# Gated RMS norm of the SSD branch: squares added on GpSimd and summed over channels once per half of the tokens, in a newly ordered instruction list

## The chip, the cores and the metric

The kernel runs on one core of a Trainium2 chip. Its time is the device time of one execution in microseconds (us). The five engines of the core (TensorE, VectorE, ScalarE, GpSimd, and SyncE for DMA issue) each run their own instruction list in order and wait for each other through semaphores. In the rows below they are called PE (with PEld for its weight loads), DVE, ACT, POOL and SP.

## The reference, cut to what matters

One layer of a hybrid network: Mamba-2 (SSD) heads and latent-attention heads side by side, a shared output projection, and a SwiGLU feed-forward part. It runs over 512 prompt tokens and 64 sample tokens, in float32. The piece that is changed is the gate of the SSD output and its RMS norm over 512 channels:

```python
y = y + p['d_skip'].astype(jnp.float32)[:, None] * xh.astype(jnp.float32)
y = y.reshape(b, T, SSD_WIDTH) * jax.nn.silu(z.astype(jnp.float32))
y_ssd = rmsnorm(y, p['ssd_norm']).astype(x.dtype)

def rmsnorm(x, w):
    xf = x.astype(jnp.float32)
    y = xf * lax.rsqrt(jnp.mean(xf * xf, axis=-1, keepdims=True) + EPS)
    return (y * w.astype(jnp.float32)).astype(x.dtype)
...
x = x + jnp.concatenate([y_ssd, o], axis=-1) @ p['w_out']
```

## The kernel before, in words

All activations lie transposed: channels on the 128 partitions, the 576 tokens (512 + 64) along the free axis. The 512 SSD channels are four tiles `xsd[:, 0..3]` of 128 x 576. The tokens are worked through in chunks of 128: chunks 0 to 3 are the prompt, chunk 4 is the 64 sample tokens. Large products are split into a high and a low float32r part and run as three matmuls of 288 columns each (`wh`/`wl` are the weights' parts); small ones run in float32, where the profile shows one matmul as two records.

The middle of the kernel, from about 95 to 215 us, has two stages that overlap. `ORDER_SSD` lists the steps of the first: `z0` to `z3` (projection of the gate, DVE line 476 reads its PSUM banks and R1), `a`, `e`, `b`, `s` (the chunk's transposes, decays, outputs, state), `g` (the gate of a chunk), `v` and `p`/`q`/`k` (values, queries and keys of head pairs). `ORDER_ATT` lists the second: `N` (the norm), `y0` to `y3` (the scaled and split operands `cat_y` of the output projection), `S`/`T`/`V` (scores, transposes, values of attention) and `F` (the part of the output projection that takes `cat_y`).

A gate (line 625) multiplies the chunk of `xsd` by `sz` on DVE (L629), squares it on ACT (L631), and sums the squares over channels on PE with a matrix of ones, into a bank of the three-bank PSUM pool `pp`. For chunks 0 to 3 the sums are packed: the 128 tokens are cut in four pieces of 32, and each piece's sums are written to 32 of the 128 partitions (L639, 16 matmuls of 32 x 32 per chunk); chunk 4 takes four matmuls of 64 columns (L636). ACT copies the result to 32 (64) columns of `ssy`, which is the buffer R1. So the norm's own arithmetic (line 815, `norm_half`, L186 to L193) runs on 192 columns in place of 576. After it, the factors have to be spread to all partitions again: four matmuls with columns of the identity (L821) and a copy of 512 columns (L825), and a 64-column copy on POOL (L818). The output `Ry` then scales `xsd` (L828), ACT writes the high part of `cat_y` (L157) and DVE the low part (L159).

The order of the instructions is not left to the order of the code. A table of numbers per engine (`ISSUE`) fixes the place of every instruction on PE, DVE, ACT, POOL and SP, and a table `PLACES` fixes which bank or buffer every tile of a pool takes.

Of the kernel before, what the change touches and what calls it, by code (L numbers as in the profile page):

```python
# [13 lines left out]
AF = mybir.ActivationFunctionType  # L14
# [5 lines left out]
P = 128  # L20
# [4 lines left out]
TH = T // 2  # L25
# [31 lines left out]
def hybrid_layer_kernel(ctx: ExitStack, tc: tile.TileContext, a, o):  # L57
# [394 lines left out]
    def bank(tag, name):  # L452
        return placed(psq if tag == "sc" else psh, [P, 512], F32, tag, name)
# [925 lines left out]
0202102121201021012012210021012101201210210120201201201201201202102102102102102102102102102102102102102102102102210120  # L1379
1202101  # L1380
# [16 lines left out]
653 657 665-667 639 689-690 668-674 640 691-704 675-676 661 677-679 705-709 658 680-681 710-712 682 644 659 683-688  # L1397
662 660 737-744 713-714 745-755 765 715-732 756-760 663 733 645-652 761 654 762 734 793 664 794 763 735 655 764 736
766-767 795-796 768-770 656 771-772 831 797-808 773-779 832 809-811 780-788 812 789-792 835 813-824 833 869-871
836-837 872 829 834 830 875 838 825-826 876 827 877 828 873-874 855-862 890 881-883 878 863 879 864-866 891 880  # L1400
887-888 867 894 884-886 868 889 895-896 926-927 897 892 928 893 929-931 898-899 839 900-904 840-844 905-909 845-852
910-913 853-854 914-921 938 947 939 922 940 923 941-942 924 943 925 932-934 948-956 935-936 957 937 958-960 993-995
944-946 1012-1013 996-997 1014 961-973 977-992 974-976 1015-1017 1002-1003 998 1004-1006 1018 999-1001 1019 1007-1011
1020-1023 1028 1024 1029 1035 1063 1051 1025-1027 1036 1064-1065 1039 1052-1053 1040-1041 1066 1054 1037 1067-1068
1055-1057 1030-1031 1069 1042-1043 1070 1044 1058-1059 1032 1060 1033 1071 1061-1062 1072 1034 1073-1074 1048-1049
# [12 lines left out]
1572-1582 1628 1647 1584 1583 1585-1590 1630 1621 1591 1622 1631 1592 1637 1593 1596-1599 1594-1595 1634 1600-1601
# [268 lines left out]
```

## Time and profile before

| what | value |
|---|---|
| median of 3 runs | 631.69 us (631.28 to 631.85) |
| profiled execution, its own time | 631.44 us |
| its span, first to last instruction | 629.5 us |
| mean granted TensorE clock | 0.997 of full speed (2.4 GHz) |
| busy: PE, DVE, ACT, POOL | 619.3, 553.6, 386.9, 75.5 us |

The span is what the trace shows; about 1.9 us of the execution's time lie around it. An engine's busy time is the union of its instructions' times, so a high share says that it always has something under way, and not by itself that it sets the end. Which engine sets the end of a stage is read from the chain of waits and from who waits for whom there.

### The profile page before, as it was taken

The numbers are of one execution on the slowest core, as the hardware profiler recorded it, in microseconds if no ns is written. First come the engines' busy times: TensorE is split into PE (matmuls) and PEld (weight loads), VectorE is DVE, ScalarE is ACT, GpSimd is POOL, SyncE is SP. The second block draws the span as 40 slices with busy tenths as digits, with TensorE's granted clock in tenths as the row PEclk, the third lists the DMA queues.
The fourth block names the chain that finished last, engine by engine and source line by source line (L and its number), as shares of the span: only waits on it lengthen the run. The fifth ranks groups of instructions, "written<-read, shape, count | busy, mean of one in ns | idle before, by whom it ended". The sixth has DMA issues, their size and how long they took to land.

```text
span 629.5 us, 12140 instructions
## 1 busy us (share of the span) xinstructions
PE 619.3 (98%) x4717; PEld 592.2 (94%) x4717; DVE 553.6 (88%) x979; ACT 386.9 (61%) x749; POOL 75.5 (12%) x113
## 2 busy tenths in 40 slices
PE   9999999999999999999999999999999999999995
PEld 9899999987787899999999999999999999999994
DVE  7899997899876799999999997799888998999676
ACT  7554335689767489756556565555665666644454
POOL 1323141011100000000012001100211011100023
PEclk9999999999999999999999999999999999999998
DMA  9512185223221223121376337460765265725105
GB/s 318 207 42 88 40 236 144 92 79 126 91 95 34 103 100 111 71 89 68 91 186 138 106 106 182 109 156 34 191 169 127 69 180 116 186 72 171 36 0 185
DMA packets 32889, 74.64 MB, mean 119 GB/s; under 512 B 3882, under 2 KB 11960, under 8 KB 32576
## 3 DMA queue, kind: packets, MB, share of 16 engines
q1 hardware_dynamic: 26688, 62.73, 30.6%
q0 software_dynamic: 5424, 10.57, 9.4%
q8 instruction: 37, 0.61, 0.4%
q10 hardware_dynamic: 720, 0.57, 0.3%
q14 instruction: 20, 0.16, 0.1%
HBM read 59.14 MB, written 4.15 MB: 101 GB/s over the span
## 4 chain that ended last, share of the span: by engine, by line
PE 83%; DVE 11%; DMA 3%; issue 2%; ACT 1%; SPq 0%; DVEq 0%; POOL 0%; ACTq 0%; POOLq 0%
PE ps_x L947 15%; PE ps_o L465 8%; PE ps_in L143 8%; PE ps_dx L1087 8%; PE ps_z L947 7%; PE ps_l L1157 4%; PE ps_y L947 4%; PE ps_dz L1087 4%; PE ps_first L143 3%; PE ps_z L465 3%; PE sc L726 3%; DMA db<-in_w_down 2%; PE ps_dy L1087 2%; PE ps_p L947 2%; PE ptp L748 1%
## 5 line engine op out<-in xcount | busy, mean ns | idle before, releaser
L947 PE MATMUL ps_x<-xop,wh_gu_S 128*128 128x288 f32 x504 | 120.0, 295 | 0.9 <-ACT u L1016 0.9
L947 PEld LDWEIGHTS ps_x<-xop,wh_gu_S 128*128 128x128 f32 x504 | 85.9, 188 | 1.6 <-ACT u L1016 1.4
L947 PE MATMUL ps_x<-xop,wl_gu_S 128*128 128x288 f32 x252 | 73.7, 295 | 0.0
L947 PE MATMUL ps_z<-xop,gu_a 128*128 128x288 f32 x252 | 57.4, 295 | 0.0
L127 ACT CAST wh_gu_S<-gu 128x1024 fp32r<-128x1024 f32 x44 | 46.0, 1052 | 16.3 <-PE ps_y L947 6.7
L128 DVE TENSOR_TENSOR wl_gu_S<-gu,wh_gu_S 128x1024 fp32r<-128x1024 f32 x44 | 53.2, 1217 | 0.9 <-ACT wh_gu_S L127 0.3
L1100 POOL DMA_DIRECT2D x<-db x16 | 14.9, 969 | 276.9 <-DVE x L1139 136.4
L947 PEld LDWEIGHTS ps_x<-xop,wl_gu_S 128*128 128x128 f32 x252 | 47.1, 188 | 0.1
L143 PE MATMUL ps_in<-xs,wh_in 128*128 128x288 f32 x256 | 45.8, 298 | 0.0
L947 PE MATMUL ps_z<-xop,wh_gu_S 128*128 128x288 f32 x168 | 42.8, 295 | 0.0
L947 PE MATMUL ps_y<-xop,wh_gu_A 128*128 128x288 f32 x168 | 42.2, 294 | 0.0
L947 PEld LDWEIGHTS ps_z<-xop,gu_a 128*128 128x128 f32 x252 | 41.8, 188 | 0.0
L947 PE MATMUL ps_x<-xop,wh_gu_A 128*128 128x288 f32 x168 | 40.2, 295 | 0.0
L143 PEld LDWEIGHTS ps_in<-xs,wh_in 128*128 128x128 f32 x256 | 37.8, 188 | 0.7 <-ACT wh_in L127 0.5
L127 ACT CAST wh_gu_A<-gu 128x1024 fp32r<-128x1024 f32 x22 | 23.1, 1051 | 17.3 <-PE ps_x L947 11.1
L465 PE MATMUL ps_o<-cat_y,wh_out 128*128 128x288 f32 x128 | 32.9, 331 | 0.0
L128 DVE TENSOR_TENSOR wl_gu_A<-gu,wh_gu_A 128x1024 fp32r<-128x1024 f32 x22 | 26.8, 1220 | 4.7 <-ACT wh_gu_A L127 2.3
L947 PEld LDWEIGHTS ps_z<-xop,wh_gu_S 128*128 128x128 f32 x168 | 29.4, 188 | 0.0
L947 PEld LDWEIGHTS ps_y<-xop,wh_gu_A 128*128 128x128 f32 x168 | 29.4, 188 | 0.1
L947 PEld LDWEIGHTS ps_x<-xop,wh_gu_A 128*128 128x128 f32 x168 | 28.7, 188 | 0.1
L143 PE MATMUL ps_in<-xs,wl_in 128*128 128x288 f32 x128 | 27.7, 295 | 0.0
L465 PE MATMUL ps_z<-xs,wh_z 128*128 128x288 f32 x128 | 26.8, 304 | 0.4 <-ACT cth L410 0.4
(610 smaller groups left out, 2005.5 us busy)
## 6 DMA issues: line engine op xcount, KB each, us to landing
gu<-in_w_gu SPq DMA_DIRECT2D x44, 512.0 KB, 4.6
db<-in_w_down SPq DMA_DIRECT2D x16, 512.0 KB, 4.6
x<-db POOLq DMA_DIRECT2D x16, 288.0 KB, 6.1
x<-dc POOLq DMA_DIRECT2D x16, 288.0 KB, 3.8
wr_in<-in_w_in SPq DMA_DIRECT2D x8, 512.0 KB, 5.2
wr_out<-in_w_out SPq DMA_DIRECT2D x8, 512.0 KB, 3.3
cumb<-cumD SPq DMA_DIRECT2D x5, 512.0 KB, 6.0
x<-in_xT SPq DMA_DIRECT2D x2, 1152.0 KB, 6.2
```

The costliest lines, as they stand in the source:

```text
L127: act.copy(hi, raw)
L128: dve.tensor_tensor(lo, raw, hi.bitcast(F32), ALU.subtract)
L143: pe.matmul(ps[:m, hf, :n], w, x[:, hf * n : (hf + 1) * n], start=start and k == 0 and i == 0, stop=stop and k == last and i == 2,)
L465: pe.matmul(ps[:, :n], w, x[:, cols], start=not onto and k == 0 and i == 0, stop=onto or (k == len(terms) - 1 and i == 2), skip_group_chec ...
L726: pe.matmul(s[:, :nk], qs[:, j, q0 : q0 + P], ks[:, j, :nk], start=True, stop=True)
L748: pe.transpose(pp[:, k : k + P], prs[p, i][:, j, b * P : b * P + P], ident)
L947: pe.matmul(ps, p, q, start=not onto and first and kp == kps[0] and j == 0, stop=onto or (last and kp == kps[-1] and j == 2), skip_group_c ...
L1087: pe.matmul(ps, l, r, start=not onto and k == 0 and j == 0, stop=onto or (k == n - 1 and j == 2), skip_group_check=onto,)
L1100: pool.dma_start(x2[t], v, accum_op=ALU.add)
L1157: pe.matmul(ps, w, x[:, cols], start=first and not onto and k == 0 and i == 0, stop=onto or (last and k == len(terms) - 1 and i == 2), ski ...
```

## The change

A gate keeps its product and its squares. The four squared channel tiles are then added on GpSimd: one instruction adds tiles 0 and 1 to tiles 2 and 3 (128 x 256 for a full chunk), a second adds the two results into the chunk's own columns of `ssy` (128 x 128). The matmuls and the copy of the gate are gone. `norm_y` sums `ssy` over channels with one float32 matmul of 288 columns per half of the tokens, and does the norm's arithmetic on each half, 288 columns wide, straight from PSUM and with the result on all partitions. The spread is gone.

```diff
@@ gate(c)
         act.activation(q, yv, AF.Square)
-        n = L // 4 if c < 4 else L
-        ps = bank("pp", f"ps_g{c}")[:, :n]
-        for t in range(4):
-            if c == 4:
-                pe.matmul(ps, ones, q[:, t], start=t == 0, stop=t == 3)
-                continue
-            for j in range(4):
-                pe.matmul(ps[32 * j : 32 * j + 32], ones[:, :32], q[:, t, j * n : j * n + n], start=t == 0, stop=t == 3)
-        act.copy(ssy[:, n * c : n * c + n] if c < 4 else ssy[:, P : P + n], ps)
+        pool.tensor_tensor(q[:, :2], q[:, :2], q[:, 2:], ALU.add)
+        pool.tensor_tensor(ssy[:, tk], q[:, 0], q[:, 1], ALU.add)
@@ norm_y()
-        R = ssy[:, : P + TS]
-        norm_half(R, R, 512)
-        pool.tensor_copy(Ry[:, TP:], R[:, P:])
-        ps = bank("pp", "ps_ry")
-        for j in range(4):
-            pe.matmul(
-                ps.rearrange("p (c j n) -> p j c n", c=4, j=4)[:, j], ident[:, 32 * j : 32 * j + 1].to_broadcast([P, P]),
-                R[:, :P].rearrange("p (c n) -> p c n", c=4), start=True, stop=True,
-            )
-        act.copy(Ry[:, :TP], ps)
+        y0, nv, u = (tmp(f"nr_y{z}") for z in "yvu")
+        for hf in range(2):
+            cols = slice(hf * TH, (hf + 1) * TH)
+            ps = bank("pp", f"ps_g{hf}")[:, :TH]
+            pe.matmul(ps, ones, ssy[:, cols], start=True, stop=True)
+            act.activation(y0[:, cols], ps, AF.Ln, scale=1.0 / 512, bias=epsb)
+            dve.tensor_scalar(nv[:, cols], ps, -0.5 / 512, -0.5 * EPS, ALU.mult, ALU.add)
+            act.activation(y0[:, cols], y0[:, cols], AF.Exp, scale=-0.5)
+            act.activation(u[:, cols], y0[:, cols], AF.Square)
+            dve.tensor_tensor(u[:, cols], u[:, cols], nv[:, cols], ALU.mult)
+            dve.scalar_tensor_tensor(Ry[:, cols], u[:, cols], 1.5, y0[:, cols], ALU.add, ALU.mult)
@@ ISSUE (PE, DVE, ACT, POOL) and PLACES["pp"]: new numbers
-0-3 7 18 28 4 8 5 9 6 10 26-27 11 29 12-17 20-22 19 23-25 31 30 32-42 54 56 58 60 55 57 59 61 43-48 50-53 49 62-75 77
+0-3 7 18 28 4 8 5 9 6 10 26-27 11 29 12-17 20-22 19 23-25 31 30 32-42 60 62 64 66 61 63 65 67 43-48 54-56 49-52 57 53
```

The lists of `ORDER_SSD`, `ORDER_ATT` and `ORDER_FFN` are as before, and so is SP's order. The new tables move instructions only in the two stages from about 95 to 215 us; the feed-forward part keeps its order. Three places follow, before and after.

PE, where the output of chunk 0 (`ps_y0`) is followed by that of chunk 1 (`ps_y1`); `ps_x2` and `ps_b2` are transposes of chunk 2, `ps_v` value tiles, `ps_s0` the state of chunk 0, `ps_g4` the sums of chunk 4's gate. Before:

```order
L573 MATMUL ps_y0_1572<-E0_1458,xdt0_1320 64x128 x8
L528 MATMUL ps_x2_1607<-ident_84,xsd_112 128x128
L657 MATMUL ps_v0_1675<-wh_uv_1670,ckv_377 128x512
L657 MATMUL ps_v0_1675<-wl_uv_1671,ckv_377 128x512
...
L657 MATMUL ps_v2_1686<-wl_uv_1671,ckv_377 128x512
L636 MATMUL ps_g4_1589<-ysq4_1587,ones_86 128x64
L657 MATMUL ps_v2_1686<-wh_uv_1670,ckv_377 128x512
L636 MATMUL ps_g4_1589<-ysq4_1587,ones_86 128x64
L657 MATMUL ps_v1_1680<-wl_uv_1671,ckv_377 128x512
L657 MATMUL ps_v1_1680<-wh_uv_1670,ckv_377 128x512
L573 MATMUL ps_y1_1642<-E1_1496,xdt1_1484 64x128 x8
```

After:

```order
L573 MATMUL ps_y0_1572<-E0_1458,xdt0_1320 64x128 x8
L573 MATMUL ps_y1_1622<-E1_1496,xdt1_1484 64x128 x8
L528 MATMUL ps_x2_1603<-ident_84,xsd_112 128x128
L507 MATMUL ps_s0_1591<-xw0_1468,bt0_1327 128x256
L650 MATMUL ps_v0_1655<-wh_uv_1650,ckv_377 128x512
L507 MATMUL ps_s0_1591<-xw0_1468,bt0_1327 128x256
```

Chunk 1's outputs stand directly behind chunk 0's; nine value matmuls, the state matmuls of chunk 0 and the gate sums of chunk 4 stood between them.

DVE, from the end of the norm to the first low part of `cat_y`; `sc` are score banks, `pr` probabilities, `qs` the queries of pair 1, and L828 (L822 after) scales a tile of `xsd` by `Ry`. Before:

```order
L711 RECIPROCAL sm_2028<-sm_2028 128x2
L676 COPY qs1_384<-ps_q1_0_1943 64x288
L716 TENSOR_SCALAR pr_0_2_2029<-pr_0_2_2029,sm_2028 128x384
L676 COPY qs1_384<-ps_q1_1_1958 64x288
L711 RECIPROCAL sm_2042<-sm_2042 128x2
L716 TENSOR_SCALAR pr_0_0_2043<-pr_0_0_2043,sm_2042 128x128
L709 TENSOR_REDUCE mx_2054<-sc0_s_2051 128x1
L828 SCALAR_TENSOR_TENSOR xsd_112<-xsd_112,par_81,Ry_1957 128x576
L709 TENSOR_REDUCE mx_2065<-sc1_3_0_2061 128x1
L828 SCALAR_TENSOR_TENSOR xsd_112<-xsd_112,par_81,Ry_1957 128x576
L709 TENSOR_REDUCE mx_2065<-sc1_3_1_2063 128x1
L159 TENSOR_TENSOR cat_y0_1998<-xsd_112,cat_y0_1998 128x576
```

After:

```order
L819 SCALAR_TENSOR_TENSOR Ry_1889<-nr_yu_1901,nr_yy_1899 128x288
L702 TENSOR_REDUCE mx_1976<-sc0_0_1_1974 128x1
L822 SCALAR_TENSOR_TENSOR xsd_112<-xsd_112,par_81,Ry_1889 128x576 x2
L704 RECIPROCAL sm_1977<-sm_1977 128x2
L669 COPY qs1_384<-ps_q1_1_1890 64x288
L704 RECIPROCAL sm_1963<-sm_1963 128x2
L709 TENSOR_SCALAR pr_0_0_1978<-pr_0_0_1978,sm_1977 128x128
L669 COPY qs1_384<-ps_q1_0_1875 64x288
L709 TENSOR_SCALAR pr_0_2_1964<-pr_0_2_1964,sm_1963 128x384
L159 TENSOR_TENSOR cat_y0_1933<-xsd_112,cat_y0_1933 128x576
```

Two of the four scalings now stand ahead of the two copies of pair 1's queries, and the maxima of pair 1 come after the first `cat_y`.

POOL, from the mask of chunk 2 on; `cumb` are the chunks' masks, `V4` a tile of values, R1 the buffer of `ssy`. Before:

```order
L545 AFFINE_SELECT cumb2_1600<-cumb2_1600 128x1024
L545 AFFINE_SELECT cumb3_1731<-cumb3_1731 128x1024
L659 MEMSET V4_1696 64x512
L818 COPY Ry_1957<-R1_99 128x64
L670 DMA qs0_382<-rrp_1163 16x576 x4
L670 DMA qs1_384<-rrp_1163 16x576 x4
```

After:

```order
L545 AFFINE_SELECT cumb2_1596<-cumb2_1596 128x1024
L632 TENSOR_TENSOR ysq4_1587<-ysq4_1587 128x128
L633 TENSOR_TENSOR R1_99<-ysq4_1587 128x64
L632 TENSOR_TENSOR ysq0_1618<-ysq0_1618 128x256
L633 TENSOR_TENSOR R1_99<-ysq0_1618 128x128
L545 AFFINE_SELECT cumb3_1711<-cumb3_1711 128x1024
L652 MEMSET V4_1676 64x512
L632 TENSOR_TENSOR ysq1_1748<-ysq1_1748 128x256
L633 TENSOR_TENSOR R1_99<-ysq1_1748 128x128
L632 TENSOR_TENSOR ysq2_1865<-ysq2_1865 128x256
L633 TENSOR_TENSOR R1_99<-ysq2_1865 128x128
L632 TENSOR_TENSOR ysq3_1860<-ysq3_1860 128x256
```

Ten additions are new (nine of them shown), in the order of chunks 4, 0, 1, 2, 3; the mask of chunk 3 (L545) stands behind the additions of chunk 0.

## Rows read from the trace of the kernel before

**Rows 1.** Busy time by stretch: start:end, length, engines (instructions), PE clock, DMA share, GB/s.

```profile
120.00:160.00 40.00, 39.96 (x382) 32.24 (x382) 38.10 (x86) 35.63 (x95) 4.18 (x7) 1.00 0.33 112
160.00:230.00 70.00, 70.00 (x525) 58.98 (x524) 51.81 (x120) 47.83 (x115) 2.11 (x4) 1.00 0.25 88
```

**Rows 2.** The chain in time order: start, us, engine, tile, line, count.

```profile
122.72 0.51 PE ps_g L636 x4
123.52 0.17 PE ps_g L636 x2
132.28 0.77 PE ps_g L639 x54
143.75 0.73 PE ps_g L639 x55
148.19 0.89 PE ps_ry L821 x8
157.69 0.13 PE ps_o L465
157.82 0.11 PE ptp_s L756
158.57 0.26 PE ps_o L465 x2
...
254.30 0.49 PE ps_n L984 x2
```

**Rows 3.** Groups on DVE, 144-262 us: count, busy us, mean ns, idle before.

```profile
L187 DVE TENSOR_SCALAR nr_v<-ps_n 128x288 f32<-128x288 f32 x1 | 0.5, 450 | 0.0
L192 DVE TENSOR_TENSOR nr_u<-nr_u,nr_v 128x288 f32<-128x288 f32 x1 | 0.4, 448 | 0.0
L193 DVE SCALAR_TENSOR_TENSOR R<-nr_u,nr_y 128x288 f32<-128x288 f32 x1 | 0.5, 459 | 0.0
L187 DVE TENSOR_SCALAR nr_v<-R 128x192 f32<-128x192 f32 x1 | 0.3, 259 | 0.4 <-ACT R L640 0.4
L192 DVE TENSOR_TENSOR nr_u<-nr_u,nr_v 128x192 f32<-128x192 f32 x1 | 0.3, 349 | 0.0
L193 DVE SCALAR_TENSOR_TENSOR R<-nr_u,nr_y 128x192 f32<-128x192 f32 x1 | 0.4, 359 | 0.0
```

**Rows 4.** DVE in time order: start, us, tile, line, idle before, releaser.

```profile
124.31 0.69 DVE L500 TENSOR_TENSOR xw<-xdt,E 128x512 f32<-128x512 f32 x1 [0.31 <-ACT E L551]
125.74 0.60 DVE L578 SCALAR_TENSOR_TENSOR xsd<-xsd,par,ps_y 128x128 f32<-128x128 f32 x2 [0.74 <-PE ps_y L573]
145.00 0.26 DVE L187 TENSOR_SCALAR nr_v<-R 128x192 f32<-128x192 f32 x1 [0.39 <-ACT R L640]
156.66 0.38 DVE L716 TENSOR_SCALAR pr<-pr,sm 128x320 f32<-128x320 f32 x1
156.96 0.75 DVE L159 TENSOR_TENSOR cat_y<-xsd,cat_y 128x576 fp32r<-128x576 f32 x1
```

**Rows 5.** Who waited for whom, 120 to 160 us: total us, times, longest.

```profile
PEld ps_y L573 <- ACT R L640: 0.4, 1, 0.4
PEld ps_o L465 <- DVE cat_y L159: 0.7, 1, 0.7
```

**Rows 6.** DVE in order of time, at 126 and 617 us.

```profile
126.27 0.68 DVE L503 TENSOR_TENSOR h<-h,el 128x512 f32<-128x512 f32 x1
...
617.46 0.42 DVE L1304 TENSOR_TENSOR sq<-sq 128x256 f32<-128x256 f32 x1
618.03 0.73 DVE L1304 TENSOR_TENSOR sq<-sq 128x256 f32<-128x256 f32 x1 [0.15 <-ACT sq L1299]
```

**Rows 7.** POOL in order of time, at the same two places.

```profile
126.61 1.30 POOL L545 TENSOR_SCALAR_AFFINE_SELECT cumb<-cumb 128x1024 f32<-128x1024 f32 x1 [12.17 <-ACT hcw L520]
...
617.49 0.98 POOL L1306 TENSOR_TENSOR ss<-ss,sq 128x256 f32<-128x256 f32 x1
```

**Rows 8.** Groups on POOL, 600 us to the end: additions of 256 columns.

```profile
L1306 POOL TENSOR_TENSOR ss<-ss,sq 128x256 f32<-128x256 f32 x4 | 3.6, 900 | 3.5 <-ACT sq L1299 3.4
```

More of the change, by code (lines that the diff above doesn't have):

```diff
@@ L1401 @@
[L1401 to L1405, printed above, removed]
@@ new lines @@
+981 996 982-983 969 960-961 970-971 984 965-967 972 997 985-987 973 998-999 974 1000 988-992 962 1001-1004 963
+1007-1012 964 1021-1022 978 1023 968 979-980 1024 975-976 1025 977 1027-1030 1026 1031-1032 1013-1014 1037-1040
+1005-1006 1015-1016 1041-1042 1017-1020 1059 1033 1060-1065 1053-1055 1066-1070 1035 1056-1058 1036 1071-1076 1034
+1046 1077-1082 1043 1099-1100 1044 1101 1045 1102-1107 1052 1049-1050 1047 1123 1083 1124 1108 1084 1125-1128 1048
+1109-1110 1085 1129 1097 1086 1130-1134 1111-1112 1051 1089 1113 1087 1219 1114 1090 1220-1221 1091 1222 1093 1115
@@ new lines @@
+1204 1276 1300 1277-1279 1301 1280-1281 1302 1282-1283 1308 1285 1309 1286 1310 1284 1303 1289 1311 1290 1304
+1291-1292 1312 1287-1288 1305 1293 1306 1294 1307 1295 1313 1326-1329 1320-1325 1330-1333 1314-1319 1334-1369
+1382-1384 1370 1385-1392 1371-1381 1393-1428 1430 1429 1431-1452 1565 1453-1459 1562 1460-1463 1553 1559 1464-1477
+1556-1557 1478-1489 1566 1563 1490-1501 1550 1554 1502-1512 1558 1577 1514-1515 1513 1516-1520 1560 1551 1521 1552
+1561 1522 1567 1523 1526-1529 1524-1525 1564 1530-1531 1586 1578 1532-1534 1583-1585 1555 1574 1538-1540 1535-1537
@@ new lines @@
+1873-1874 1893-1899 1912 1878-1883 1875 1913 1884-1886 1914-1915 1924-1928 1900-1902 1948 1929 1949 2002 1903-1908
+1916-1917 1887 1930-1931 1909-1910 1932-1933 2003-2004 1911 1934 1950 2005-2006 1951 2007 1952 1936-1939 1935
+1918-1923 1953 2020 2032-2034 1940-1945 1954 2021 1946 1990-1993 1978-1979 1947 1980-1981 2035 1955-1957 1982-1983
+2022-2024 1994 2036 1966-1968 1958-1959 1984 1996-1997 2026-2027 1985 1998 1969 1995 2025 1960 1986 2028 1970 2037
+2029 1971 1961 1999-2000 1987-1988 1972-1974 1989 2030-2031 1975-1976 2044 2001 2045 2038-2040 2056 1977 1962
@@ new lines @@
+2041-2043 2057-2058 2046-2048 2014 1963-1964 2008-2009 2049-2051 1965 2010 2015 2062 2052-2054 2063 2055 2059-2060
+2064-2066 2011-2012 2016 2013 2068 2092 2061 2093 2069 2067 2094-2099 2070-2071 2017-2018 2080-2081 2019 2100
+2072-2079 2101 2170 2082-2089 2104-2106 2116 2102 2107-2111 2117-2118 2090-2091 2112 2119 2171 2103 2113-2115
+2172-2173 2120-2121 2174 2122-2126 2158-2159 2134-2138 2160 2146-2147 2139 2175 2140-2144 2127-2131 2148-2149 2188
+2200-2201 2150 2189-2193 2152 2161 2132-2133 2194 2151 2206 2153 2145 2207 2195 2162 2154-2156 2208-2209 2202 2157
@@ new lines @@
+2342-2343 2352-2354 2358-2361 2380 2362 2381-2383 2363-2364 2368-2372 2365-2367 2384 2373-2379 2355 2392-2402
+2385-2386 2404-2406 2387-2388 2403 2407 2389 2408 2416 2452 2417 2453 2418-2421 2409 2428-2429 2422 2390 2423
+2410-2412 2391 2454 2413-2414 2430-2431 2415 2424 2455-2456 2506-2507 2425 2440-2443 2508 2444 2457 2445-2447
+2426-2427 2448-2450 2432-2436 2451 2509-2511 2458-2462 2482 2437 2494 2483 2438 2536 2463-2465 2470 2484 2439 2466
+2524 2471-2472 2525-2526 2473 2485 2495 2474 2486-2487 2475 2496 2467 2476 2527 2488-2490 2500-2501 2477 2497 2478
@@ new lines @@
+3447 3458 3518 3459 3519 3467 3502 3468 3503 3469-3471 3490 3504 3472 3478 3532 3479 3473-3474 3491-3492 3475
+3480-3481 3533-3534 3493 3482-3483 3544 3494-3495 3545 3484-3487 3476 3505 3477 3538 3508 3496 3506-3507 3497 3539
+3509 3535 3488 3498 3546 3540 3499-3500 3489 3501 3510 3547 3536 3548 3511-3512 3537 3541-3542 3520 3556 3521 3513
+3522 3557 3550 3543 3551 3523-3524 3552 3558 3553 3559 3554-3555 3560 3525 3568 3561 3569 3526 3549 3562-3563
+3570-3571 3527 3564-3566 3528-3529 3567 3572 3592-3593 3530-3531 3573 3594 3574-3575 3595-3596 3576 3580 3597
@@ new lines @@
+4029-4030 4006 4031-4033 4007 4012 4008 4034 4009-4011 4013-4018 4035-4038 4049 4019 4050-4052 4020-4023 4053
+4039-4043 4060 4044-4047 4061 4054-4058 4062 4059 4072-4075 4063-4065 4076-4077 4108 4066 4078-4079 4067-4069
+4096-4097 4109-4113 4098-4099 4080-4082 4084-4085 4100-4101 4086 4102 4114 4070 4087 4083 4103-4105 4071 4106-4107
+4088-4091 4115-4116 4132-4133 4092-4095 4156 4165 4117-4118 4134-4136 4120-4125 4119 4137 4126 4166 4138 4127-4129
+4174 4139 4167 4140 4130-4131 4183 4157 4141 4158 4142-4148 4175-4176 4149 4159 4177 4216-4217 4184-4185 4150-4152
@@ new lines @@
+4186 4218 4187 4204 4153 4205 4168 4160 4178 4161 4154-4155 4179 4276 4169 4219 4277 4180 4206 4188 4181 4170-4171
+4278-4279 4189 4172 4207 4173 4190 4182 4162 4220 4208-4211 4198 4280 4240-4242 4191 4201 4199 4221 4163 4243 4200
+4164 4192 4202 4222-4225 4195-4196 4193 4244 4212 4194 4226-4227 4203 4245-4247 4197 4213-4215 4313-4315 4281
+4228-4231 4252 4316-4317 4248 4232-4235 4264-4265 4318 4236 4319 4237-4238 4266-4267 4320 4239 4249 4268-4269
+4250-4251 4253 4270 4282 4321 4283 4271-4274 4254-4257 4289-4290 4301 4275 4291 4284 4302 4285-4288 4258-4261 4303
@@ L1550 @@
+914 920 913 912 921 898 924 933 922-923 934 927-928 939 935 892 925 929 926 930-931 936 932 937 940 946 938 941 943
+942 945 944 947-948 950 949 951-952 954 956 959 955 953 957-958 960 962 965 961 963 969 966 970 964 967-968 972 971
+973-981
 """,
```

295 lines of the change are left out of this document (128 added, 167 removed).

## The prediction

> **What bounds the kernel now.** The windows come first, because the change moves instructions only between about 95 and 215 us. From 120 to 160 us PE is busy 39.96 of 40 us and DVE 38.10; from 160 to 230 us PE is busy all of 70.00 us and DVE only 51.81 [rows 1]. The granted clock is 1.00 in both, so nothing here turns on the clock. The chain of waits, read next, lies on PE throughout these stretches, and the gate's sums and the spread stand in it with their own times [rows 2]. That reads as if every PE instruction removed came back as time. The waits say otherwise: PE's load for the output projection waits 0.7 us for `cat_y` from DVE [rows 5], and the last low part of `cat_y` ends at 157.71 (156.96 + 0.75) [rows 4], 1.12 us before the projection's last matmul ends at 158.83 (158.57 + 0.26) [rows 2]. So the stretch up to 158.8 us has two engines that are almost full, and PE's end there cannot come earlier than DVE's last `cat_y` plus the matmuls that need it. Behind it PE alone sets the time, and whatever is won or lost at 158.8 us is passed on to the end of the kernel. The rest of the kernel keeps its order.
>
> **The change, part by part.**
>
> PE. Removed are the sums of chunk 4 (0.51 + 0.17 + 0.17 = 0.85 us in three pieces, the two short ones alike), those of chunks 0 to 3 (0.77 + 0.73 = 1.50) and the spread (0.89): 3.24 us [rows 2]. Added are two float32 matmuls of ones by 288 columns. The feed-forward norm has the same one, 0.49 us in two records [rows 2], so 0.98. Net -2.26 us of PE, all ahead of the projection's end. Nothing else is moved across that end but two transposes of `ptp_s`, which now stand behind it.
>
> DVE. Removed are the three norm instructions of 192 columns, 0.259 + 0.349 + 0.359 = 0.97 us; added are two sets of 288 columns, 2 x (0.450 + 0.448 + 0.459) = 2.71 [rows 3]. That is +1.74 by durations. DVE starts the next instruction a little before the last one is through: the scaling of `pr` at 156.66 lasts 0.38, and its successor starts 0.30 later [rows 4]. With 0.08 off for each of three more instructions, the addition is +1.50. That same scaling of `pr` is the one instruction that now comes after the last low part: -0.30. Everything else ahead of the last `cat_y` is the same set in another order, the two scalings of `xsd` ahead of the queries' copies included.
>
> DVE's waits. Three of before can go: 0.31 for the exponentials of a chunk, 0.74 for `ps_y` and 0.39 for the packed sums' copy [rows 4], 1.44 us together. The 0.74 stands beside PE's 0.4 us wait of `ps_y` for ACT's copy of the gate sums, which frees the bank [rows 5]; that copy is gone, and chunk 1's outputs now stand directly behind chunk 0's. The 0.39 was for the copy of the last gate; now the first half needs only chunks 0 to 2, whose sums are early. What is late next is the second half: square, two additions, matmul. Behind chunk 3's product DVE has eight other instructions (four maxima, a split, the first half's first norm instruction and two for `pr`) before it asks for the second half's sums. They have to cover the square on ACT, two additions (about 1.35, below) and the matmul (0.49). I take it that they do, and all 1.44 as gone; the bounds are 0 and the additions' whole 1.35, nearer to 0 for eight instructions. DVE's sum is -1.44 + 1.50 - 0.30 = -0.24 us for the last low part of `cat_y`.
>
> ACT. The packed copy and the copy of the spread go, and its norm work grows from 192 columns to twice 288. ACT is busy 35.63 of 40 us [rows 1] and is not asked for directly by the end of the stretch; I cost it at nothing, covered by DVE's own work. If that cover fails, it shows as a wait of DVE's L818 for ACT, and I bound it by the 0.39 us that DVE waited for ACT at the norm before [rows 4], on either side of zero.
>
> POOL. Ten additions. Additions of 128 x 256 take 0.90 us on average here [rows 8]; by columns I estimate 0.45 for 128 x 128 and 0.23 for 64 columns, so 4 x 1.35 + 0.68 = 6.1 us, on an engine that is busy 4.18 of 40 us [rows 1]. Its own time costs nothing. Its effect on DVE may: two additions of 256 columns on DVE, the same instruction twice, took 0.42 us at 617.46 and 0.73 at 618.03, and during the second POOL's own addition (617.49, 0.98 us) was running [rows 6, 7]. The other way round, POOL's mask at 126.61 took 1.30 us beside DVE's product of 0.68 [rows 6, 7], so DVE does not lose each time. One meeting costs DVE 0.31 us. Bounds: nothing, if every addition falls beside DVE instructions that don't mind, up to ten meetings, 3.1 us. I take one meeting, 0.31, and set against it the 0.46 us of DVE's idle time in the stretch (40 - 38.10 - 1.44) that I did not count; neither enters the sum.
>
> The Trainium skill, "SBUF — State Buffer", section "Who interferes with whom", has a rule against this change: VectorE and GpSimd share a port pair, a VectorE instruction with two SBUF inputs contends with a GpSimd instruction that reads SBUF, and whoever issued first holds the lock for its whole instruction. The pair of 0.42 and 0.73 us agrees with it. By the rule every two-input DVE instruction that follows an addition waits out its rest, and the sum would be that of the second rival; by the mask at 126.61 POOL pays, and the sum stays.
>
> The tail. After the last low part, PE has about six matmuls of 0.13 us and one transpose of 0.11 left [rows 2], 0.89 us against 1.12 before; but that transpose now waits for the scaling of `pr` that DVE does after the last `cat_y` (0.38), which brings it back to at most 1.1. I take 0.95: -0.17 us. The two transposes moved behind the end cost 2 x 0.11 = +0.22.
>
> Sum: -0.24 - 0.17 + 0.22 = -0.19 us. Of PE's 2.26 us the rest turns into waiting for `cat_y`. From the profiled execution's 631.44 us (its span of 629.5 and 1.9 around it) that is 631.25; the median of the runs is 0.25 above the profiled one, so about 631.5. What PE may still lose for want of bank or order is a few tenths either way; the likeliest case spans 630.5 to 632.4.
>
> **The rivals.**
>
> *PE sets the end after all.* The chain stands on PE throughout and PE waits for `cat_y` only 0.7 us in all [rows 2, 5]. If DVE's waits are due to PE's lateness, and not to DVE's own load, all of PE's 2.26 us comes back, less 0.22 for the transposes: -2.04, 631.69 - 2.04 = 629.7 us. Against it: DVE has only 1.90 us of idle time in the 40 us, and gains 1.2 us of work (1.50 - 0.30). For this rival, DVE would have to lose its idle time entirely and its queue to run shorter than the durations say, or what it does late would have to be needed late.
>
> *POOL's additions hold DVE up.* About half of DVE's work in the stretch has two SBUF inputs (the gate's product, the carried state, the low parts, the scalings). Half of POOL's 6.1 us on such instructions is 3.05; of the 0.44 us by which the addition at 617.49 overlapped its neighbour at 618.03, DVE lost 0.31, 0.7 of it [rows 6, 7]: 2.1 us. With -0.19 that is +1.9, 633.6 us. It decides from about 1.4 us on, that is from five meetings. For it: DVE is the engine without slack, and the additions fall right behind the gates' products, where DVE goes on with the next chunk. Against it: much of what follows there reads PSUM, and POOL also gives way.
>
> *The second half comes late.* The sums matmul stands in PE's queue between the scores of pair 0, and if POOL's two additions are not through, the scores behind it wait as well, and DVE's maxima after them. At 0.3 to 1.3 us (1.3 being the second half's two additions in full) this gives 631.8 to 632.8, and lies mostly within the likeliest case.
>
> **How the numbers follow.** Likeliest case, including a late second half: 0.52. PE sets the end: 0.28. POOL holds DVE up: 0.20. A difference of 0.2% of 631.69, or 1.26 us, is about what can be told from none; so the first case is "same" but for small tails, the second "faster" and the third "slower". Faster 0.29, same 0.51, slower 0.20. The range leaves out the far half of each rival: from 629.4, a little below the faster rival's point, to 633.2, short of the slower one's.
>
> **What would show it.** In the chain after: two `ps_g` pieces of 0.49 us, no spread, `ps_y1` straight behind `ps_y0`. On DVE the idle times of 0.31, 0.74 and 0.39 are gone, and six norm instructions of 0.45 stand ahead of the scalings. If I am right, PE waits longer than 0.7 us for `cat_y` or for DVE just ahead of it, and the projection ends within 0.5 us of 158.8. If `cat_y` ends at 156 or earlier, the first rival holds. If DVE's two-input instructions (L503, L586, L629, the splits) take 0.9 us or more where an addition runs on POOL, and there are five or more such, the second does. A wait of PE's L465 or of the scores for POOL shows the third. A difference in the feed-forward part, from 230 us on, would make the whole account wrong.

## The result, and the profile after

The changed kernel takes 632.83 us (median of 22 runs, 631.39 to 633.37) where the kernel before takes 631.65 (22 runs, 631.14 to 632.39): a ratio of 1.0016, with an interval of 1.0010 to 1.0022. It is slower by about 1 us; the forecast was 631.5 and a difference of -0.2. The time lies inside the stated range (629.4 to 633.2), above the likeliest case's upper end of 632.4, and the change has the other sign.

Single executions of one kernel differ by up to 2 us (631.39 to 633.37), which is more than the effect. So the stretch that the change touches is measured by itself: from the start of the last activation of `cth` (ACT, L410) to the start of the first sums matmul of the feed-forward norm (PE). The rows of the timeline (start, duration, engine, line) of the kernel before, of the changed kernel, and of the changed kernel profiled once more:

```profile
94.27 0.69 ACT L410 ACTIVATE cth<-cacc 128x579 f32<-128x579 f32 x1 [0.86 <-DVE cacc L408]
...
254.14 0.65 PE L984 MATMUL ps_n<-fz,ones 128*128 128x288 f32 x2
```

```profile
94.89 0.69 ACT L410 ACTIVATE cth<-cacc 128x579 f32<-128x579 f32 x1 [1.37 <-DVE cacc L408]
...
255.59 0.65 PE L978 MATMUL ps_n<-fz,ones 128*128 128x288 f32 x2
```

```profile
94.32 0.69 ACT L410 ACTIVATE cth<-cacc 128x579 f32<-128x579 f32 x1 [0.51 <-DVE cacc L408]
...
255.01 0.65 PE L978 MATMUL ps_n<-fz,ones 128*128 128x288 f32 x2
```

Subtracted, these give 159.87 us before, 160.70 after, 160.69 after once more. The stretch is longer by 0.83 us and repeated to 0.01 in the one pair of profiles that there is of one kernel (the kernel before was profiled once), while in the two profiles of one and the same kernel the part ahead of it differs by 0.57 us (94.89 and 94.32) and the part from its end to the last instruction by 0.54. This length, and not the time of a whole profile, is the measure of what follows. The time to the end of the last low part of `cat_y` is counted from the same start (63.44 us before, 63.66 after); it is a mark in DVE's list.

Busy time over this stretch, before and after, columns as in [rows 1]:

```profile
94.27:254.14 159.87, 159.41 (x1299) 139.51 (x1297) 133.47 (x283) 119.90 (x293) 9.87 (x14) 1.00 0.30 99
94.89:255.59 160.70, 158.28 (x1159) 136.85 (x1158) 135.07 (x286) 120.73 (x290) 16.40 (x23) 1.00 0.30 99
```

PE has lost 1.13 us of busy time (159.41 to 158.28), half of the 2.26 foretold, and its idle time has grown by 1.96, from 0.46 (159.87 - 159.41) to 2.42 (160.70 - 158.28); together these are the 0.83. DVE has gained 1.60, and POOL went from 9.87 to 16.40. What answers to [rows 2], from the chain of the changed kernel (start, us, what):

```profile
119.76 1.90 PE ps_y L573 x32
143.11 0.79 ACT pr L703 x2
...
144.67 0.77 PE ps_g L813 x2
145.46 0.51 ACT nr_yy L814
145.99 0.46 DVE nr_yv L815
...
149.67 1.45 DVE xsd L822 x2
151.12 0.09 DVE sm L704
151.23 0.41 ACT pr L707
...
159.41 0.53 PE ps_o L465 x4
```

Chunk 1's outputs stand behind chunk 0's (32 records in one piece), the packed sums and the spread are gone, and the second half's sums are in the chain with 0.77 us, where the feed-forward norm's have 0.49 [rows 2]. Between 143 and 149 us the chain now goes from ACT to PE to ACT to DVE, where it lay on PE before. PE ends the projection at 159.94 (159.41 + 0.53). Where PE now stands idle (in brackets), and the wait of its loads for POOL, to be set beside [rows 5]:

```profile
143.94 0.70 PE L719 MATMUL sc<-ks,qs 100*128 100x256 f32 x2 [0.42 <-ACT pr L703]
149.94 1.12 PE L719 MATMUL sc<-ks,qs 100*128 100x512 f32 x2 [0.26 <-ACT qs L669]
151.79 1.10 PE L719 MATMUL sc<-ks,qs 100*128 100x512 f32 x2 [0.73 <-ACT pr L707]
```

```profile
PEld ps_g L813 <- POOL R L633: 0.7, 2, 0.4
```

With two more, ahead of queries (0.35, for DVE's copy) and of a chunk's outputs (0.16, for DVE's decays), these are 1.92 us. All stand ahead of scores, queries and outputs, and none is for `cat_y`. The last one is the end of a chain: two scalings of `xsd` on DVE, DVE's reciprocal, ACT's scaling of the probabilities (L707), and the scores that PE does next (releasers are inferred from semaphore events). From there, 151.79, PE has no idle time of 0.1 us or more up to the end of the stretch, which comes 103.80 us later. So in the changed kernel the last low part of `cat_y` at 158.56 is not what PE waits for.

And DVE, in order of time, where it meets POOL:

```profile
128.11 1.39 DVE L586 TENSOR_TENSOR xsd<-xsd,ecp 128x512 f32<-128x512 f32 x1
140.67 0.89 DVE L586 TENSOR_TENSOR xsd<-xsd,ecp 128x512 f32<-128x512 f32 x1
141.59 0.83 DVE L629 TENSOR_TENSOR xsd<-xsd,sz 128x512 f32<-128x512 f32 x1
143.54 0.76 DVE L128 TENSOR_TENSOR wl_pair<-wr_pair,wh_pair 128x384 fp32r<-128x384 f32 x1
```

```profile
127.86 1.09 POOL L545 TENSOR_SCALAR_AFFINE_SELECT cumb<-cumb 128x1024 f32<-128x1024 f32 x1
...
140.27 0.73 POOL L632 TENSOR_TENSOR ysq<-ysq 128x256 f32<-128x256 f32 x1 [6.13 <-ACT ysq L631]
141.09 0.78 POOL L633 TENSOR_TENSOR R<-ysq 128x128 f32<-128x128 f32 x1
143.16 0.72 POOL L632 TENSOR_TENSOR ysq<-ysq 128x256 f32<-128x256 f32 x1 [1.29 <-ACT ysq L631]
```

Read the two together. The sum into `xsd` at 128.11 began while POOL's mask ran (to 128.95) and ended 0.55 us after it, at 129.50. The next one began at 140.67, during the addition that ended at 141.00, and ended 0.56 after that. The third began during the addition that ended at 141.87 and ended 0.55 after it; the split at 143.54 met the addition that ended at 143.88 and ended 0.42 after. Four instructions of 0.69, 0.69, 0.69 and 0.55 us (their durations elsewhere in this trace) have become 1.39, 0.89, 0.83 and 0.76: 1.25 us more.

A meeting of this kind stood in the trace of the kernel before as well, ahead of the window of [rows 1]:

```profile
113.68 1.37 DVE L480 SCALAR_TENSOR_TENSOR sz<-zt,zh 128x576 f32<-128x576 f32 x1
113.35 1.09 POOL L545 TENSOR_SCALAR_AFFINE_SELECT cumb<-cumb 128x1024 f32<-128x1024 f32 x1 [5.09 <-ACT el L520]
```

The product took 1.37 us where others of its form take 0.74, and ended 0.61 after the mask. In the changed kernel no instruction with two SBUF inputs falls on that mask any more (L480 is done at 108.82). The new order so ends one meeting of 0.63 us with a mask and makes another of 0.70; whether the one that went had cost time is not shown, since DVE is idle around that place.

### The profile page after: what moved, and what is told of

Same layout as the page of the kernel before. It is cut to its first block, busy times and chain, and to the rows that moved or that the text cites. A ratio compares the mean times of both kernels' runs of the same rounds, so it can differ in the third digit from the quotient of the medians.

```text
span 631.2 us, 11878 instructions
## 1 busy us (share of the span) xinstructions
PE 618.6 (98%) x4577; PEld 590.3 (94%) x4577; DVE 555.1 (88%) x982; ACT 387.7 (61%) x746; POOL 81.9 (13%) x122
## 3 DMA queue, kind: packets, MB, share of 16 engines
q1 hardware_dynamic: 26688, 62.73, 30.6%
## 4 chain that ended last, share of the span: by engine, by line
PE 80%; DVE 14%; DMA 3%; issue 2%; ACT 1%; SPq 0%; DVEq 0%; ACTq 0%
PE ps_x L941 15%; PE ps_in L143 8%; PE ps_dx L1081 8%; PE ps_o L465 8%; PE ps_z L941 8%; PE ps_l L1151 4%; PE ps_dz L1081 4%; PE ps_y L941 4%; PE ps_first L143 3%; PE ps_z L465 3%; DMA db<-in_w_down 2%; PE sc L719 2%; PE ps_dy L1081 2%; PE ptp L741 2%; PE pv L766 1%
```

## The experiments

Each ratio is that of 11 runs (9 for "before, with the ten additions", 5 for "scalings late", 10 for "48 sums fewer", whose eleventh took 1226 us and is not counted) to runs of the kernel before on the same chip, with its interval of 95%. "Stretch" is the length defined above (159.87 before, 160.70 after) and "low part" is the time to the end of the last low part of `cat_y` (63.44, 63.66), both from the run's profile. Three theories were on record: 1, POOL's additions hold DVE up; 2, the new order keeps PE waiting; 3, the wider norm loads DVE.

| kernel | ratio (interval) | low part | stretch |
|---|---|---|---|
| changed, once more | 1.0009 (1.0000 to 1.0018) | 63.65 | 160.69 |
| changed, additions of two columns | 0.9994 (0.9985 to 1.0003) | 62.97 | 159.98 |
| before, with the ten additions | 1.0026 (1.0017 to 1.0036) | 65.37 | 161.79 |
| changed, scalings late | 1.0035 (1.0021 to 1.0049) | 65.07 | 162.17 |
| changed, DVE's norm cut | 0.9995 (0.9986 to 1.0004) | 63.26 | 160.37 |
| changed, ACT's norm cut | 1.0002 (0.9993 to 1.0010) | 63.36 | 160.41 |
| changed, both cut | 0.9992 (0.9984 to 1.0001) | 62.55 | 159.60 |
| before, norm 576 wide | 1.0021 (1.0012 to 1.0030) | 65.48 | 161.87 |
| before, 48 sums fewer | 0.9986 (0.9977 to 0.9995) | 63.38 | 159.81 |
| changed, POOL set apart | 0.9990 (0.9982 to 0.9999) | 62.95 | 160.02 |
| the same, split early | 1.0000 (0.9991 to 1.0009) | 63.26 | 160.31 |
| the same, split behind | 1.0003 (0.9994 to 1.0012) | 62.73 | 160.18 |

The ratios hold the ends of the execution as well, where nothing was changed, so two kernels whose stretches differ by 0.2 us can stand in either order by their ratios. In all twelve rows the time, taken from the ratio, lies 0.1 to 0.8 us lower against the kernel before than the stretch says; only the first result lies higher, by 0.2. The cause of this is open, and the 159.87 rests on one profile. So differences between stretches are trusted here among variants, and one of 0.2 us or less to the kernel before is taken for none.

In the changed kernel, its repetition and six variants (additions of two columns, the three norm cuts, POOL set apart, split early) the time from the end of PE's wait at the scores (151.79 above) to the end of the stretch is 103.78 to 103.87 us. What a variant gains or loses it has gained or lost by then; the low part moves along, because DVE does both out of one list.

**The changed kernel once more.**

> The changed kernel itself, once more, on the same chip as the others of this call, to have its ratio and its profile beside theirs. All theories: slower than the kernel before by 0.8 to 1.2 us, a ratio of 1.0013 to 1.002, and between the table's cosine exponential at 95 us and the projection's end the same times as in its first profile, within 0.05 us.

1.0009 is below the range expected, which its interval still reaches; the stretch repeated to 0.01 us. ("The table's cosine exponential" in that text is the activation of `cth`.)

**The additions taken away, or put into the kernel before.** The first kernel leaves all but two columns of each sum out:

```diff
-        pool.tensor_tensor(q[:, :2], q[:, :2], q[:, 2:], ALU.add)
-        pool.tensor_tensor(ssy[:, tk], q[:, 0], q[:, 1], ALU.add)
+        pool.tensor_tensor(q[:, :2, :2], q[:, :2, :2], q[:, 2:, :2], ALU.add)
+        pool.tensor_tensor(ssy[:, c * P : c * P + 2], q[:, 0, :2], q[:, 1, :2], ALU.add)
```

> The changed kernel with GpSimd's ten additions cut to two columns each: same instructions, order and waits, but only two columns of each chunk are added and the other columns of the sums are left as they were. Theory 1 (the additions hold up DVE's two-input instructions by the shared port, 0.20 + 0.14 + 0.21 us at chunks 2 and 3 and part of the 0.70 us at L586): time falls by 0.5 to 1.2 us against the changed kernel's 632.83, to 631.6 to 632.3, and L586, L629 and the split at 140 to 144 us return to 0.69, 0.69 and 0.55. Theory 2 (the new order on DVE makes PE wait for pair 1): the PE waits of 0.5 and 0.9 us at 150 to 152 us stay, and the time stays within 0.3 of 632.8.

The stretch lost 0.72 us and the low part 0.69. The same four DVE instructions as above:

```profile
128.39 1.15 DVE L586 TENSOR_TENSOR xsd<-xsd,ecp 128x512 f32<-128x512 f32 x1
140.73 0.69 DVE L586 TENSOR_TENSOR xsd<-xsd,ecp 128x512 f32<-128x512 f32 x1
141.45 0.69 DVE L629 TENSOR_TENSOR xsd<-xsd,sz 128x512 f32<-128x512 f32 x1
143.26 0.56 DVE L128 TENSOR_TENSOR wl_pair<-wr_pair,wh_pair 128x384 fp32r<-128x384 f32 x1
```

The mask of chunk 3 in that run:

```profile
127.91 1.09 POOL L545 TENSOR_SCALAR_AFFINE_SELECT cumb<-cumb 128x1024 f32<-128x1024 f32 x1 [1.05 <-ACT hcw L520]
```

Three are back at 0.69, 0.69 and 0.56; the first still meets the mask. What they gave back is 0.24 + 0.20 + 0.14 + 0.20 = 0.78 us, all but 0.09 of which reached `cat_y`. Short additions are also done sooner, and the sums' matmul no longer waits for POOL in this run; what separates the two is the next kernel, in which nothing reads the additions, and the one with POOL's work set apart, in which all of them run. Theory 1 holds, and the additions alone are the difference between 159.98, which no run could tell from the kernel before, and 160.70. The counterpart, in the kernel before (results unused):

```diff
         act.activation(q, yv, AF.Square)
+        j2, j1 = sz[:, :2, tk], sz[:, 2, tk]
+        pool.tensor_tensor(j2, q[:, :2], q[:, 2:], ALU.add)
+        pool.tensor_tensor(j1, j2[:, 0], j2[:, 1], ALU.add)
```

> The kernel before with the ten additions of the change put onto GpSimd as well, in the place that they have in the changed kernel; nothing reads their results (they go into columns of sz that the gates no longer need). Theory 1: the additions alone make the kernel before slower by 0.5 to 1.5 us, in DVE's L586, L629, L503 and the splits. Rivals 2 and 3: they cost nothing, since nobody waits for them; within 0.3 us of the kernel before.

Slower by 1.9 us in the stretch, and all of it at `cat_y` already (63.44 to 65.37). DVE and POOL of that kernel:

```profile
132.12 0.69 DVE L606 TENSOR_TENSOR h<-h,ps_s 128x512 f32<-128x512 f32 x1 [0.65 <-PE ps_s L507]
132.73 1.22 DVE L128 TENSOR_TENSOR wl_out<-wr_out,wh_out 128x1024 fp32r<-128x1024 f32 x1
133.86 1.23 DVE L503 TENSOR_TENSOR h<-h,el 128x512 f32<-128x512 f32 x1
...
143.29 0.98 DVE L586 TENSOR_TENSOR xsd<-xsd,ecp 128x512 f32<-128x512 f32 x1
144.30 0.83 DVE L629 TENSOR_TENSOR xsd<-xsd,sz 128x512 f32<-128x512 f32 x1
```

```profile
132.96 1.58 POOL L633 TENSOR_TENSOR sz<-ysq 128x256 f32<-128x256 f32 x1 [2.65 <-ACT ysq L631]
...
142.99 0.72 POOL L633 TENSOR_TENSOR sz<-ysq 128x256 f32<-128x256 f32 x1 [7.59 <-ACT ysq L631]
143.80 0.78 POOL L634 TENSOR_TENSOR sz<-sz 128x128 f32<-128x128 f32 x1
```

L503 began at 133.86 during an addition that ended at 134.54 and ended 0.55 after it (135.09); the other two ended 0.56 and 0.55 after theirs. The addition at 132.96 was itself held by the split of 1.22 us that DVE had begun at 132.73, and lasted 1.58 where others of its size take 0.72. But meetings are not the whole of the 1.9 us, which is more than the 0.5 to 1.5 expected. The mask of chunk 3 now stands behind chunk 0's additions, and ACT waits for it:

```profile
129.77 0.40 ACT L551 ACTIVATE E<-cumb,ncum 128x128 f32<-128x128 f32 x1 [0.96 <-POOL cumb L545]
```

Behind this wait ACT's copy of values is late, PE is idle for 0.74 us at 130.69 for that copy, and DVE for 0.65 at 132.12 for the state. By the end of that instruction (L606) the kernel is 0.99 us behind the kernel before, counted from the same start (37.97 against 36.98); the other 0.94 come behind it, at the meetings shown and at a split (0.77 in place of 0.55), less 0.28 of idle time that they take up. So, as the profile has it, in this order the ten additions cost about 1.0 us through the mask that waits behind them and 0.9 through meetings, in the new order 0.7.

**POOL's work set apart.** All additions run; ACT squares chunk 2 ahead of the table load, and POOL fills the value tile ahead of the mask:

```diff
 ACT   L673 ks (pair 0)
+ACT   L631 ysq of chunk 2
 ACT   L552 ecp
 ACT   L682 table load
-ACT   L631 ysq of chunk 2
...
+POOL  L652 memset V4
 POOL  L545 mask of chunk 3
-POOL  L652 memset V4
```

> The changed kernel with two instructions moved so that GpSimd's work falls beside DVE instructions that read PSUM. ACT squares chunk 2 before the table load and the exponential of chunk 3's ecp, so that its additions run at 138.3 to 139.8 us beside the queries' copy and the L578 group; and GpSimd fills the value tile before it masks chunk 3, so that DVE's L586 at 128.1 us starts first. All additions still run. Theory 1 (DVE's two-input instruction waits for the end of GpSimd's instruction and only then runs, for about 0.55 us more): L586 at 128 us goes from 1.39 to about 0.7, L586 and L629 at 141 us from 0.89 and 0.83 to 0.69, and the time falls by 0.6 to 1.1 us against the changed kernel's, to a ratio of 1.000 or below to the kernel before. If the additions cost by their number or by PE's wait for them, nothing moves.

The stretch fell by 0.68 to 160.02, as expected, with all additions running.

```profile
127.60 0.68 DVE L586 TENSOR_TENSOR xsd<-xsd,ecp 128x512 f32<-128x512 f32 x1
128.80 0.98 DVE L629 TENSOR_TENSOR xsd<-xsd,sz 128x512 f32<-128x512 f32 x1
139.76 0.69 DVE L586 TENSOR_TENSOR xsd<-xsd,ecp 128x512 f32<-128x512 f32 x1
140.49 0.69 DVE L629 TENSOR_TENSOR xsd<-xsd,sz 128x512 f32<-128x512 f32 x1
142.29 0.81 DVE L128 TENSOR_TENSOR wl_pair<-wr_pair,wh_pair 128x384 fp32r<-128x384 f32 x1
```

```profile
127.46 0.52 POOL L652 MEMSET V<- 64x512 f32 x1
128.06 1.18 POOL L545 TENSOR_SCALAR_AFFINE_SELECT cumb<-cumb 128x1024 f32<-128x1024 f32 x1
137.42 0.73 POOL L632 TENSOR_TENSOR ysq<-ysq 128x256 f32<-128x256 f32 x1 [4.03 <-ACT ysq L631]
138.23 0.46 POOL L633 TENSOR_TENSOR R<-ysq 128x128 f32<-128x128 f32 x1
```

The additions at 137.42 to 138.69 lie beside the queries' copy and the L578 group, which read PSUM and keep their times (0.46 and 0.34 to 0.35), and the two instructions behind them are at 0.69. POOL's fill at 127.46, which reads nothing, did not hold the sum that began at 127.60 (0.68). The mask, to 129.24, now meets the product at 128.80 (+0.29), and the split still meets the last addition. By its ratio of 0.9990 this kernel is 0.6 us faster than the kernel before (0.1 to 1.1); its stretch is 0.15 us longer, so I take the two as equal. Two attempts at the split that remained:

```diff
-DVE   L128 split of pair 2's weights, behind the two maxima of 512
+DVE   the same, ahead of L606 at 137.7 us            (first)
+DVE   the same, behind the last cat_y and the pr of L709   (second)
```

> The kernel with the two moves of GpSimd's neighbours, and a third: DVE's split of pair 2's weights goes from 143.5 us, where it meets the last chunk's addition (0.76 in place of 0.55), to 137.7 us, ahead of the state's sum. Theory 1: 0.2 us less than with the two moves alone, and faster than the kernel before by 0.2 to 0.6 us. If the order around it matters more (the states and the scores come 0.5 us later), 0.2 to 0.5 us more.

> The changed kernel with the two moves that set GpSimd's work apart from DVE's two-input instructions, and DVE's split of pair 2's weights (0.81 us at 142.3 us there, beside the last chunk's addition) put behind the last low part of cat_y and the scaling of pr. Theory 1 with DVE and its partners in one chain up to cat_y: the split's 0.73 us leave the chain, cat_y and the projection end 0.4 to 0.7 us earlier than with the two moves alone, and the kernel is faster than before by 0.6 to 1.2 us, a ratio of 0.998 to 0.999. If PE's queue at the split's use (ps_q of pair 2) gets late, or PE's own backlog sets the projection's end, 0.2 us or less.

Neither gained. The first made the stretch 0.29 longer, the second of the two cases expected: the split went in front of the last state and gate, and PE was idle for 0.41 us ahead of `ps_i` for that state, which it is not with POOL set apart alone. The second was a miss: it brought the low part 0.22 forward, less than expected, and the stretch came out 0.16 longer. The split then stood in front of the sums that free the projection's banks (L797), and the chain up to 165 us of that run goes from the split at 157.51 over L797 at 158.44 to PE's queries at 158.87. I take this for the cause; no run tested it.

**Who sets the end of the stretch.** In the kernel before, 48 of the 64 sums matmuls left out (only `t == 0` is summed):

> The kernel before with 48 of the 64 matmuls of the packed sums left out (only the first of the four channel tiles of chunks 0 to 3 is summed): about 1.1 us less PE work, and nothing else moves. If PE's own work sets the end of the stretch (my first rival), the time falls by 0.8 to 1.1 us. If DVE does (the forecast), it falls by 0.4 us at most.

The low part moved by 0.06 us and the stretch by 0.06. Its busy time over the stretch:

```profile
95.03:254.84 159.81, 158.85 (x1202) 138.52 (x1201) 133.52 (x283) 119.82 (x293) 9.85 (x14) 1.00 0.30 99
```

PE did 0.56 us less work than in the kernel before (159.41) and was idle for 0.50 more (0.96 against 0.46). So PE's work is covered there, as the forecast said, and 48 sums were worth 0.56 us and not the 1.1 expected, which is three quarters of the 1.50 that the chain's pieces last. Its ratio, 0.9986, says 0.9 us faster (0.3 to 1.5), which is what the first rival foretold for this run; the profile shows no place for it in the stretch, and that contradiction stays open. Next, the norm of the changed kernel with DVE's part cut, ACT's part cut, and both:

```diff
+            cn = slice(hf * TH, hf * TH + 2)
-            dve.tensor_scalar(nv[:, cols], ps, -0.5 / 512, -0.5 * EPS, ALU.mult, ALU.add)
-            dve.tensor_tensor(u[:, cols], u[:, cols], nv[:, cols], ALU.mult)
+            dve.tensor_scalar(nv[:, cn], ps[:, :2], -0.5 / 512, -0.5 * EPS, ALU.mult, ALU.add)
+            dve.tensor_tensor(u[:, cn], u[:, cn], nv[:, cn], ALU.mult)
...
-            act.activation(y0[:, cols], y0[:, cols], AF.Exp, scale=-0.5)
-            act.activation(u[:, cols], y0[:, cols], AF.Square)
+            act.activation(y0[:, cn], y0[:, cn], AF.Exp, scale=-0.5)
+            act.activation(u[:, cn], y0[:, cn], AF.Square)
```

> The changed kernel with two of the three DVE instructions of the norm in each half cut to two columns (the correction step of the norm is left out for the other columns); the instructions, their order and their waits stay. DVE's load ahead of cat_y falls by four times about 0.35, 1.4 us. Theory 3 (DVE's load, with 2.71 us of norm in place of 0.97, sets the end of the stretch): the last low part of cat_y ends 1.0 to 1.4 us earlier and the time falls by 0.7 to 1.4 us. Theory 2 (PE's waits behind the order, through ACT): 0.3 us or less.

> The changed kernel with two of the three ACT instructions of the norm in each half cut to two columns (the exponential and the square are left out for the other columns; DVE multiplies other numbers): ACT loses about 1.3 us of work between 145 and 148 us. If ACT's load at the norm, which I costed at nothing, holds PE's score banks and so the end of the stretch, the time falls by 0.4 to 1.2 us. If DVE's load sets it, it moves by 0.3 us at most.

> The changed kernel with both engines' norm work cut: on DVE two of three and on ACT two of three instructions of each half work on two columns (the other columns are not corrected and hold the logarithm). DVE alone cut gave 0.4 us at cat_y, ACT alone 0.3. If the norm is a chain that runs through both engines, the two together give their sum or more, 0.7 to 1.5 us; if some third wait (the scores' banks, the reciprocal) holds it, no more than 0.5.

0.40, 0.30 and 1.11 us at the low part. So theory 3 was wrong in size: 1.2 us of DVE's work taken away (four instructions that went from 0.45 to 0.16 us, 0.15 for two of them) gave 0.4. At the norm DVE and ACT feed each other, and cutting one leaves the other; cutting both gives more than the two alone. The width alone, put into the kernel before (`norm_half(ssy, ssy, 512)` on 576 columns):

> The kernel before with one part of the change alone: the norm's arithmetic on 576 columns in place of 192 (the extra columns hold old numbers that nobody uses), three instructions on DVE and three on ACT, each about 0.4 us longer on DVE. The forecast priced the width at 1.5 us of DVE. If the norm's width is on the chain of the stretch, 1 to 2.5 us slower than the kernel before (both engines' instructions follow each other); if the neighbours cover it, 0.5 or less.

2.0 us slower, at `cat_y` already. Its chain, at the norm:

```profile
146.00 0.66 ACT nr_y L186
147.12 0.58 ACT nr_y L188
147.73 0.69 ACT nr_u L189
148.45 0.77 DVE nr_u L192
149.24 0.76 DVE R L193
```

The five steps follow each other through ACT and DVE, 3.5 us in one row. In the changed kernel the two halves overlap, which may be why its norm, 2 x 288 wide, costs less than this one; no run separates that.

**The order on DVE.** The first two scalings behind the reciprocals and the queries' copies again:

> The changed kernel with one move on DVE: the first two scalings of xsd stand behind the reciprocals, the queries' copies and the small probabilities of pair 0 again, as they did in the kernel before. Theory 2 (these two scalings, 1.45 us, in front of the reciprocal keep PE waiting 0.5 us for the queries' bank and 0.9 us for a score bank): both waits go, PE comes to the projection with less behind it, and the time falls by 0.4 to 1.0 us. Theory 1 and theory 3 (DVE's own load sets the end of cat_y): the last low part ends where it did and the time stays within 0.3 us.

Theory 2 fell, with the sign reversed: the stretch grew by 1.5 us and the low part by 1.4. The scalings had filled time in which DVE otherwise waits: without them it was idle for 0.61 us ahead of the reciprocal, and twice for 0.2 us for ACT's high parts of `cat_y`. PE lost the wait of 0.73 us at the scores and got one of 1.55 ahead of the transposes, for the probabilities. So the wait that the changed kernel's end follows is real, but putting the scalings late is no way to take it out.

## Why the prediction was wrong, point by point

- **That DVE paces the stretch and PE's gain turns into waiting: right in kind, wrong in size and place.** PE's busy time fell by 1.13 us in the stretch, not 2.26, and the time did not follow; without 48 sums the kernel before moved by 0.06 us. By the stretch the first rival (PE sets the end) fell with that. The 2.26 was worked out from the chain's pieces, and leaving matmuls out gave less than their pieces last: 48 sums came to 0.56 us of busy time where the pieces say 1.1. The waiting is not for `cat_y`, as foretold, but for ACT and DVE ahead of scores, queries and outputs, the last of it over at 151.79. "DVE" was too narrow a name: at the norm it is DVE and ACT in turn, and ACT's longer norm, which I had at nothing, is part of it (0.30 us alone, 1.11 with DVE's).
- **DVE's sum, -0.24 us for the last low part: right but for POOL.** Without the additions it came 0.47 us earlier than before; with them, 0.22 later. The sum began at 120 us, so the meeting with the mask at 113.68, which the new order ends, was not in it. The three waits of [rows 4] went as foretold.
- **POOL's additions: the step that failed.** "I take one meeting, 0.31, and set against it the 0.46 us of DVE's idle time", with neither in the sum: the additions cost 0.72 us. There were three meetings with additions and a worse one with the mask of chunk 3 (0.70), which in the new order falls on L586; 0.46 of that is left when the additions are cut, since the mask then waits for its input from ACT, and I had not looked at what it would meet. A meeting does not cost a fixed 0.31: DVE's instruction waits out what is left of POOL's and then runs on for about 0.55 us. The row that I set against it, POOL's mask of 1.30 us at 126.61 [rows 7], is the same rule from the other side: DVE's product had begun at 126.27 [rows 6], first. The Trainium skill, "SBUF — State Buffer", section "Who interferes with whom", says that whoever issued first holds the port for the whole instruction; the eight DVE rows of 128 x 512 shown here, and the addition of 1.58 us, agree. The prediction quoted that rule and then weighed it as one of two readings, by the one mask that DVE had met first; the mask at 113.35 in the same trace, beside which L480 took 0.63 us longer, shows the other side. Taken at its word, with the places where POOL's additions would fall read from the order (right behind each gate's square), it could have given the sign.
- **The second rival: its mechanism, not its size.** It was put at 1.9 us from five meetings on; four made 1.25 us on DVE, and the additions' share was 0.72 at the end of the stretch. In the kernel before's order the same additions cost 1.9, about half of it through a mask that came late and not through meetings.
- **The tail and the moved transposes: +0.05 us in the sum, +0.60 in the profile.** PE's last projection matmul ended 1.38 us after the last low part (159.94 against 158.56), where I had 0.95 and the kernel before 1.12. The term built on "PE waits for `cat_y`" was the wrong path: PE works without a wait from 151.79 on and comes to the last low part with the projection's work still queued. What is left up to the end of the stretch, the two transposes and the order of what follows, is +0.34 against +0.22.
- **The late second half: small.** PE's loads of the two halves' sums waited for POOL, 0.7 us in two waits, and PE itself was not idle ahead of these matmuls.

Summed over the stretch: foretold -0.19, measured +0.83. The 1.02 between them are 0.72 of additions and 0.55 of tail and transposes, less 0.23 that DVE's part did better, to 0.02. This is bookkeeping by the low part, not the path that PE waited on. Without the additions the change would have been no difference that can be told, which is what the forecast said; that the rest comes so near is partly luck, since PE's saving was half of what was foretold and the tail came out otherwise.

## What to carry to other kernels

An instruction given to an idle GpSimd is free only if no VectorE instruction with two SBUF inputs begins while it runs, and if nothing that others wait for stands behind it on GpSimd. Where VectorE is on the path, read from the order which instructions these will be, and put GpSimd's work beside instructions that read PSUM (here copies, maxima and sums with an input in PSUM, which kept their times). Moving two neighbours gave back 0.68 us of 0.83 here. And where an effect is of the size of the run-to-run spread, measure the stretch that was changed between two fixed instructions, which repeated to 0.01 us, and split it into the busy and the idle time of the engine at its end, which says where a saving went.

## What the runs showed of the hardware that was not expected

- A VectorE instruction that begins during a GpSimd instruction ends 0.54 to 0.56 us after that one's end, for 128 x 512 sums and products that take 0.68 to 0.69 us alone, whether GpSimd adds (five rows) or masks (three): most of the instruction runs after the wait. The 384-column split ended 0.42 after in the changed kernel.
- GpSimd's additions of 128 x 256 take 0.72 to 0.73 us when undisturbed and up to 1.58 when VectorE was first (behind a split of 1.22 us that ended at 133.95, this one ended 0.59 later).
- 48 of the packed sums' matmuls, about 1.1 us in the chain, took only 0.56 us of TensorE's busy time with them when they were left out.
- The same kernel's execution differed by 0.57 us ahead of the stretch and 0.54 behind it in two profiles, and by 0.01 within it.
